# Diagonal masks on TensorE, the forget gate's place, and the order of emptying queries and keys in a two-branch attention layer

## The chip, the cores and the metric

The kernel runs on one core of a Trainium2 chip. The metric is the device time of one execution in microseconds (us), the median of several runs. A core has five engines with a queue of instructions each: TensorE (PE) for matmuls, VectorE (DVE), ScalarE (ACT), GpSimd (POOL), and SyncE (SP), which here only starts transfers. An engine runs its queue in order; engines wait for each other through semaphores. TensorE writes its results into eight PSUM banks of 128 x 512 floats, and ACT and DVE empty them.

## The reference

One decoder layer on 512 tokens of width 1024. Its mixing part has two causal attention branches of 8 heads with 64 channels each, forgetting attention (FoX) and stick-breaking attention (SB):

```
mod = c @ w_ada + b_ada                 # shift, scale and gate for both parts
u = x * (1.0 + sc1) + sh1
q_a, k_a, v_a, f_a, q_b, k_b, v_b, g_a, g_b = split(u @ w_in)
log_f = log_sigmoid(f_a + b_forget);  cum = cumsum(log_f)
y_fox = softmax(where(s <= t, q k^T / 8 + cum_t - cum_s, -inf)) @ v
z = q k^T / 8                                               # stick-breaking
log_one_minus = where(s < t, log_sigmoid(-z), 0)
rest = cumsum(log_one_minus, reversed over s) - log_one_minus
y_sb = where(s < t, exp(log_sigmoid(z) + rest), 0) @ v
merged = sigmoid(g_a) * (y_fox @ w_fox_proj) + sigmoid(g_b) * (y_sb @ w_sb_proj)
x = layer_norm(alpha * x + (1.0 + gt1) * (merged @ w_o))
...
```

After it comes a gated MLP with a causal depthwise convolution of width 3, and a second layer norm. Everything is in float32.

## The kernel before

Each float32 operand is split into a high part of reduced precision (`wh`, `uh`, `s`, `m`; ACT copies it, L75) and a low part, the rest (`wl`, `ul`; DVE subtracts, L78). A product is then three matmuls, high x high, low x high and high x low (L116 to L118).

The program has four stretches. Up to about 52 us the modulation is worked out and the first block of projections runs (L270). Up to about 300 us the attention runs. Then come the output projection and layer norm, the up projection (L116 to L118 on `u2h`), the down projection (L984 to L986) and the last norm.

The attention goes through 16 heads, the 8 SB heads first (pairs 0 to 3), then the 8 FoX heads (pairs 4 to 7). Each head has three stages. Stage a (L446) computes scores from `s` (queries) and `m` (keys) into three banks (L454 and L455). For an SB head ACT then takes two sigmoids, of -z into `om` and of z into `pt` (L487, L488); POOL sets the diagonal blocks of `pt` to zero above and on the diagonal (L490); DVE scans `om` from right to left for the running products (L493), and POOL multiplies (L494). For a FoX head four matmuls with `mska` (L460) add -1e30 above the diagonal, and a softmax follows. Stage b (L504) transposes the ten blocks of `pt` (L514) into three banks, which ACT empties into `ph`, `ptc` (high) and DVE into `pl`, `ptc` (low). Stage c (L527) multiplies by the values (L532); ACT and DVE add the two halves (`ytmp` L538, `yf` L539), and after a pair split the sum into `yh` and `yl`.

Between these stages `fill` pulls matmuls out of a `stream` of independent work: projections of queries and keys of later pairs, of the branch gates (`proj`), values (`vproj`, `vgroup`), the branches' output products (`bproj`), and two row sums of the modulation (`ada_sum`, L584 and L585, whose operands `ach` and `acl` are split by `ada_split`). `fill` takes a fixed number of triples (`FILL`), and the stream must have reached the next pair's keys before that pair's scores. Up to head 6's turn the stream stops ahead of `vgroup`, the values of the FoX heads, whose four banks are filled side by side with 96 matmuls (L428 to L430).

The stream's weights are items in one list. SP loads them in that order into four raw buffers, and DVE and ACT split them one or two items ahead of their use. Between them stand 24 modulation pieces (`add_ada`): the first 8 are added up on DVE in two `ac` sums (L561, L566), the others reduced against c (L170). `skip` counts how many places for a piece stay empty at first. The first two items (`EARLY`) are held back behind a given instruction. SP runs in the order of the code; the order on the four other engines is set by a scheduler from the dependencies, with `issue_after` as a hint, so a change in one place moves instructions in others.

`q_evac` and `k_evac` empty a pair's projection bank: rows 0 to 63 are the first head, rows 64 to 127 the second. ACT and DVE take turns on a bank. `forget` (the Abs, Exp and Ln of the forget gate on ACT, each with its table; its scan L328 and its split `chi` on DVE; rows sent into `s` and `m` of the FoX heads by POOL's transfers) is called ahead of head 4's turn.

Of the kernel before, what the change touches and what calls it, by code (L numbers as in the profile page):

```python
# [8 lines left out]
F32 = mybir.dt.float32  # L9
F32R = mybir.dt.float32r  # L10
BF16 = mybir.dt.bfloat16
AF = mybir.ActivationFunctionType
ALU = mybir.AluOpType
# [3 lines left out]
P = 128  # L17
# [9 lines left out]
NEG = -1.0e30  # L27
# [18 lines left out]
def layer_kernel(ctx: ExitStack, tc: tile.TileContext, out, xT, x, cT, crow, wa0, wa1, bcol, bgt, w1, wct, wv, bf,  # L46
# [3 lines left out]
    V, S, G, PE = nc.vector, nc.scalar, nc.gpsimd, nc.tensor  # L50
# [14 lines left out]
    def bank():  # L65
        return pp.tile([P, 512], F32, name=nm("ps"), tag="ps")

    def const(shape, dt, s):
        return cons.tile(shape, dt, name=s, tag=s)

    def fl(ap):
        return ap.bitcast(F32)
# [4 lines left out]
    def lo_of(o, i, hi):  # L77
        return V.tensor_tensor(o, i, fl(hi), ALU.subtract)  # L78
# [20 lines left out]
    identb = const([P, P], BF16, "identb")  # L99
    V.tensor_copy(identb, ident)  # L100
    zerob = const([P, P], BF16, "zerob")
    G.memset(zerob, 0.0)
    mska = const([P, P], BF16, "mska")
    G.affine_select(mska, zerob, pattern=[[-1, P]], compare_op=ALU.is_ge, fill=NEG, base=0, channel_multiplier=1)
    one = const([P, 512], F32, "one")
    G.memset(one, 0.0)
    G.affine_select(one[:, 384:512], one[:, 384:512], pattern=[[-1, P]], compare_op=ALU.is_gt, fill=1.0, base=0, channel_multiplier=1)
    bfs = const([NH, 1], F32, "bfs")
    modc = const([P, 4, KT], F32, "modc")
    modr = const([P, 4, KT, 2], F32, "modr")  # L110
# [11 lines left out]
    state = {"load": 0, "proc": 0}  # L122
# [17 lines left out]
    def process():  # L140
        it = items[state["proc"]]
        if state["proc"] < EARLY:
            with tc.issue_after(state["after"].ins):
                it[4] = it[1](it[3])
        else:
            it[4] = it[1](it[3])
        state["proc"] += 1
# [151 lines left out]

    OFS = ((0, 0), (2, 0), (0, 128), (1, 0))  # L300
    SEG = (((0, 128), (128, 512)), ((0, 512),), ((0, 256),))
    ptc = [[att.tile([P, 512], F32R, name=f"ptc{i}{e}", tag=f"ptc{i}{e}") for e in range(2)] for i in range(2)]
    for e in ptc:
        for t in e:
# [2 lines left out]
    m2t = [att.tile([68, 512], F32R, name=f"m2_{i}", tag=f"m2_{i}") for i in range(4)]  # L307
# [37 lines left out]
    hd = {}  # L345
# [3 lines left out]
    def slot_free(n):  # L349
        assert n < 4 or n - 4 in scored  # L350
        return n % 4

    def idx(br, h):
        return h if br == 1 else NH + h

    def q_evac(br, p, ps):
        for hh in range(2):
            h = 2 * p + hh
            r = slice(64 * hh, 64 * hh + 64)
            s1 = z(F32R, "s1")  # L360
            hi_of(s1[0:64, :], ps[r, :], 0.125)
            V.scalar_tensor_tensor(s1[64:128, :], ps[r, :], 0.125, fl(s1[0:64, :]), ALU.mult, ALU.subtract)
            d = hd.setdefault((br, h), {})
            d["s1"] = s1
            if br == 0:
                s2 = s2t[slot_free(idx(br, h))]
                hi_of(s2[0:64, :], ps[r, :], 0.125)
                d["s2"] = s2
            else:
                d["s2"] = s1  # L370

    def k_evac(br, p, ps):
        for hh in range(2):
            h = 2 * p + hh
            r = slice(64 * hh, 64 * hh + 64)
            m1 = z(F32R, "m1")
            hi_of(m1[0:64, :], ps[r, :])
            hi_of(m1[64:128, :], ps[r, :])
            m2 = m2t[slot_free(idx(br, h))]
            lo_of(m2[0:64, :], ps[r, :], m1[0:64, :])  # L380
            d = hd.setdefault((br, h), {})
            d["m1"], d["m2"] = m1, m2

    def v_evac(br, j, half, ps):
        vv = z(F32R, "vv")
# [59 lines left out]

    def stage_a(br, h):  # L446
        d = hd[(br, h)]
        bk = [bank(), bank(), bank()]

        def scores(i):  # L450
            b, o = OFS[i]
            w = max(256, (i + 1) * P)
            tb = slice(i * P, (i + 1) * P)
            PE.matmul(bk[b][:, o : o + w], d["s1"][:, tb], d["m1"][:, 0:w], start=True, stop=False)  # L454
            PE.matmul(bk[b][:, o : o + w], d["s2"][0:68, tb], d["m2"][0:68, 0:w], start=False, stop=br == 1)  # L455

        def mask(i):
            b, o = OFS[i]
            if br == 0:
                PE.matmul(bk[b][:, o + i * P : o + i * P + P], identb, mska, start=False, stop=True)  # L460

        scores(0)
        mask(0)
        scores(2)
        scores(1)
        scores(3)
        mask(2)
        mask(1)
        mask(3)
        pt = [z(F32, "pt"), z(F32, "pt"), z(F32, "pt")]  # L470
        if br == 0:
            sm = att.tile([P, 12], F32, name=nm("sm"), tag="sm", bufs=3)
            for i in (0, 2, 1, 3):
                b, o = OFS[i]
                c = slice(o, o + (i + 1) * P)
                V.tensor_reduce(sm[:, i : i + 1], bk[b][:, c], AX.X, ALU.max, negate=True)
                S.activation(pt[b][:, c], bk[b][:, c], AF.Exp, bias=sm[:, i : i + 1], accum_out=sm[:, 4 + i : 5 + i])
            V.reciprocal(sm[:, 8:12], sm[:, 4:8])
            for i in (0, 2, 1, 3):
                b, o = OFS[i]  # L480
                c = slice(o, o + (i + 1) * P)
                V.tensor_scalar_mul(pt[b][:, c], pt[b][:, c], sm[:, 8 + i : 9 + i])
        else:
            for b in (0, 2, 1):
                w = SEG[b][-1][1]
                om = z(F32, "om")
                S.activation(om[:, 0:w], bk[b][:, 0:w], AF.Sigmoid, scale=-1.0)  # L487
                d["last"] = S.activation(pt[b][:, 0:w], bk[b][:, 0:w], AF.Sigmoid)  # L488
                dg = pt[b].rearrange("p (a c) -> p a c", c=P)[:, (0, 3, 1)[b] : w // P : 3, :]
                G.affine_select(dg, dg, pattern=[[0, dg.shape[1]], [-1, P]], compare_op=ALU.is_gt, fill=0.0, base=0, channel_multiplier=1)  # L490
                for s, e in SEG[b]:
                    d0 = om[:, s + 1 : e][:, ::-1]
                    V.tensor_tensor_scan(d0, d0, one[:, 513 - (e - s) : 512][:, ::-1], 1.0, ALU.mult, ALU.max)  # L493
                    G.tensor_tensor(pt[b][:, s : e - 1], pt[b][:, s : e - 1], om[:, s + 1 : e], ALU.mult)  # L494
        d["pt"] = pt
        scored.add(idx(br, h))
        if br == 0 and h + 4 < NH:
            decay_rows(h + 4)
        if br == 1 and h >= 4 and gated:
            decay_rows(h - 4)  # L500
# [136 lines left out]
    stream, sums = [], []  # L637
    adas = [0]

    skip = [7]  # L640

    def add_ada(n=1):
        for _ in range(n):
            if skip[0]:
                skip[0] -= 1
            elif adas[0] < 24:
                add_item(wa1[adas[0]], ada_proc(adas[0]))
                adas[0] += 1
                if adas[0] in (4, 8):
                    stream.append((ada_split, (adas[0] // 4 - 1, len(items) - 1)))  # L650
                    sums.append([len(stream) + 1, adas[0] // 4 - 1])
# [34 lines left out]
    for p, ng in ((1, 0), (2, 0), (3, 2), (4, 1)):  # L686
        if p == 4:
            marks["v0"] = len(stream)
            for j in range(4):
                stream.append((vgroup, (j, add_item(wv[0, j], split_proc))))  # L690
                add_ada(2)
        add_pair(p)
        if p == 1:
            for j in range(4):
                wvi.append(add_item(wv[1, j], v_proc))
            for j in range(NB):
                stream.append((vproj, (1, j, wvi[-1])))
            marks["v1"] = len(stream)
        for _ in range(ng):
            add_gate(1, gb.pop(0))  # L700
# [80 lines left out]
    heads = [(br, 2 * p + e) for br, p in seq for e in range(2)]  # L781
    last = hd[heads[1]]['last']
    for n, (b, h) in enumerate(heads):
        if n == 4:
            forget(last)
        f1, f2, f3 = FILL[n // 8]
        if n + 2 < 16:
            if n == 6:
                lim[0] = marks["y1"]
            if n % 2 == 0:  # L790
                fill_to(marks[(n // 2 + 1, "k")])
            last = hd[heads[n + 1]].get("last")
            stage_a(*heads[n + 2])
        fill(f1)
        if n + 1 < 16:
            stage_b(*heads[n + 1])
        fill(f2)
        if n == 0:
            fill_to(marks["v1"])
        stage_c(b, h)  # L800
        if n == 7:
            lim[0] = marks["y0"]
        if n == 15:
            lim[0] = len(stream)
        fill(f3)
# [98 lines left out]
    hh, hl = [], []  # L904
# [34 lines left out]
    for n in range(2 * FT):  # L939
        if n < NSPLIT:  # L940
            h, l = items[wui[n]][4]
            ps = bks[n]
            up_mm(ps, h, l, slice(256, 512))
        else:
            ps = bank()
            h, l = weights(wui[n])
# [13 lines left out]
        if n % 2 == 1:  # L960
# [4 lines left out]
            a, b = z(F32R, "hh"), z(F32R, "hl")  # L965
# [23 lines left out]
    for j in range(FT - LATE):  # L989
        w = weights(wdi[j])  # L990
# [4 lines left out]
    for i in range(NB):  # L995
        tb = slice(i * P, (i + 1) * P)
        r = x1[i]
# [96 lines left out]
```

## Time and profile before

| what | value |
|---|---|
| median of three runs (770.62, 772.75, 772.47) | 772.47 us |
| the profiled execution | 773.12 us |
| its span, first to last instruction | 771.4 us |
| mean granted TensorE clock | 0.994 |
| TensorE busy | 752.7 us |
| DVE, ACT, POOL busy | 546.5, 350.9, 197.9 us |

The 1.7 us between the profiled execution and its span lie before the first and after the last instruction. A row of a timeline gives start, duration, engine, line, operation, output <- inputs and shapes; "x3" means that three equal rows in a row are taken together, and brackets give the time in which the engine stood idle just before, with what ended it. The program's names stand without their numbers.

### The profile page before, as it was taken

The numbers are of one execution on the slowest core, as the hardware profiler recorded it, in microseconds if no ns is written. First come the engines' busy times: TensorE is split into PE (matmuls) and PEld (weight loads), VectorE is DVE, ScalarE is ACT, GpSimd is POOL, SyncE is SP. The second block draws the span as 40 slices with busy tenths as digits, with TensorE's granted clock in tenths as the row PEclk, the third lists the DMA queues.
The fourth block names the chain that finished last, engine by engine and source line by source line (L and its number), as shares of the span: only waits on it lengthen the run. The fifth ranks groups of instructions, "written<-read, shape, count | busy, mean of one in ns | idle before, by whom it ended". The sixth has DMA issues, their size and how long they took to land.

```text
span 771.4 us, 9543 instructions
## 1 busy us (share of the span) xinstructions
PE 752.7 (98%) x3538; PEld 622.3 (81%) x3538; DVE 546.5 (71%) x816; ACT 350.9 (45%) x587; POOL 197.9 (26%) x162
## 2 busy tenths in 40 slices
PE   8999999898999999999999999999999999999995
PEld 4877888786888888888889888888888888888885
DVE  6868668988789885776676787677656665534666
ACT  3568468725867555433145434444444433222300
POOL 1037236920100011363000780000000043945500
PEclk9999999999999999999999999999999999999999
DMA  8952310378332323455302524344332214322302
GB/s 330 405 181 82 110 56 28 111 243 274 112 113 92 121 86 123 155 166 163 137 1 71 204 76 146 119 178 137 112 106 93 100 54 165 122 96 88 105 27 83
DMA packets 31106, 99.68 MB, mean 129 GB/s; under 512 B 4274, under 2 KB 4786, under 8 KB 31059
## 3 DMA queue, kind: packets, MB, share of 16 engines
q1 hardware_dynamic: 30258, 98.72, 37.3%
q8 instruction: 28, 0.46, 0.3%
q10 hardware_dynamic: 288, 0.28, 0.1%
q0 software_dynamic: 512, 0.07, 0.1%
q14 instruction: 20, 0.16, 0.1%
HBM read 96.88 MB, written 2.10 MB: 128 GB/s over the span
## 4 chain that ended last, share of the span: by engine, by line
PE 83%; DVE 7%; ACT 5%; DMA 3%; issue 2%; DVEq 0%; ACTq 0%
PE ps L116 16%; PE ps L117 16%; PE ps L118 16%; PE ps L985 5%; PE ps L986 5%; PE ps L984 5%; PE ps L270 4%; PE ps L532 2%; PE ps L864 2%; PE ps L863 2%; PE ps L865 2%; PE ps L514 2%; DVE wl L78 1%; PE ps L454 1%; DVE om L493 1%
## 5 line engine op out<-in xcount | busy, mean ns | idle before, releaser
L78 DVE TENSOR_TENSOR wl<-raw,wh 128x1024 fp32r<-128x1024 f32 (+2 forms) x106 | 147.1, 1389 | 92.4 <-ACT wh L75 91.9
L75 ACT ACTIVATE wh<-raw 128x1024 fp32r<-128x1024 f32 (+2 forms) x106 | 110.3, 1042 | 98.7 <-PE ps L986 38.3
L116 PE MATMUL ps<-u2h,wh 128*128 128x512 f32 (+1 forms) x376 | 141.4, 376 | 0.0
L117 PE MATMUL ps<-u2l,wh 128*128 128x512 f32 (+1 forms) x376 | 141.3, 376 | 0.0
L118 PE MATMUL ps<-u2h,wl 128*128 128x512 f32 (+1 forms) x376 | 141.3, 376 | 0.0
L624 POOL TENSOR_TENSOR raw<-raw,gt 128x1024 f32<-128x1024 f32 x22 | 59.7, 2727 | 190.8 <-DVE gt L587 157.7
L117 PEld LDWEIGHTS ps<-u2l,wh 128*128 128x128 f32 x376 | 70.8, 188 | 12.9
L116 PEld LDWEIGHTS ps<-u2h,wh 128*128 128x128 f32 x376 | 70.8, 188 | 12.8
L118 PEld LDWEIGHTS ps<-u2h,wl 128*128 128x128 f32 x376 | 70.8, 188 | 12.6
L116 PE MATMUL ps<-uh,wh 128*128 128x512 f32 x200 | 79.7, 399 | 0.0
L117 PE MATMUL ps<-ul,wh 128*128 128x512 f32 x200 | 78.5, 392 | 0.0
L118 PE MATMUL ps<-uh,wl 128*128 128x512 f32 x200 | 78.4, 392 | 0.0
L985 PE MATMUL ps<-wl,hh 128*128 128x512 f32 x128 | 49.9, 390 | 0.0
L986 PE MATMUL ps<-wh,hl 128*128 128x512 f32 x128 | 49.8, 389 | 0.0
L984 PE MATMUL ps<-wh,hh 128*128 128x512 f32 x128 | 49.8, 389 | 0.0
L118 PEld LDWEIGHTS ps<-uh,wl 128*128 128x128 f32 x200 | 37.7, 189 | 8.1
L116 PEld LDWEIGHTS ps<-uh,wh 128*128 128x128 f32 x200 | 37.8, 189 | 7.1
L117 PEld LDWEIGHTS ps<-ul,wh 128*128 128x128 f32 x200 | 37.9, 189 | 6.9
L75 ACT ACTIVATE hh<-cv 128x512 fp32r<-128x512 f32 x22 | 13.9, 632 | 59.8 <-DVE cv L964 59.8
L612 POOL TENSOR_TENSOR raw<-raw,gt 128x1024 f32<-128x1024 f32 x8 | 19.9, 2498 | 78.2 <-DMA raw<-in_wo 47.2
L963 ACT ACTIVATE cv<-cv 128x512 f32<-128x512 f32 x22 | 13.9, 632 | 54.6 <-DVE cv L958 54.6
L494 POOL TENSOR_TENSOR pt<-pt,om 128x127 f32<-128x127 f32 (+3 forms) x32 | 34.5, 1088 | 1.8
(192 smaller groups left out, 1532.3 us busy)
## 6 DMA issues: line engine op xcount, KB each, us to landing
raw<-in_wup SPq DMA_DIRECT2D x44, 512.0 KB, 3.3
raw<-in_wa SPq DMA_DIRECT2D x32, 512.0 KB, 3.4
raw<-in_wct SPq DMA_DIRECT2D x25, 512.0 KB, 4.0
raw<-in_wdn SPq DMA_DIRECT2D x22, 512.0 KB, 3.3
wa<-in_wa SPq DMA_DIRECT2D x14, 512.0 KB, 7.9
raw<-in_wv SPq DMA_DIRECT2D x8, 512.0 KB, 3.9
raw<-in_wp SPq DMA_DIRECT2D x8, 512.0 KB, 3.4
raw<-in_wo SPq DMA_DIRECT2D x8, 512.0 KB, 3.2
```

The source lines that it names most:

```text
L75: S.activation(o, i, AF.Copy, scale=scale)
L78: return V.tensor_tensor(o, i, fl(hi), ALU.subtract)
L116: PE.matmul(ps, wh, ah, start=first, stop=False)
L117: PE.matmul(ps, wh, al, start=False, stop=False)
L118: PE.matmul(ps, wl, ah, start=False, stop=last)
L270: PE.matmul(grp[g], w, u, start=j == 0 and n == 0, stop=j == KT - 1 and n == (1 if g == 7 else 2))
L494: G.tensor_tensor(pt[b][:, s : e - 1], pt[b][:, s : e - 1], om[:, s + 1 : e], ALU.mult)
L612: G.tensor_tensor(r, r, gt[0], ALU.mult)
L624: G.tensor_tensor(r, r, gt[1], ALU.mult)
L984: PE.matmul(ps, hh[j][:, tb], w[0], start=first, stop=False)
L985: PE.matmul(ps, hh[j][:, tb], w[1], start=False, stop=False)
L986: PE.matmul(ps, hl[j][:, tb], w[0], start=False, stop=last)
```

## The change

The diff, cut to its core:

```diff
-    one = const([P, 512], F32, "one")
-    G.memset(one, 0.0)
-    G.affine_select(one[:, 384:512], one[:, 384:512], pattern=[[-1, P]], compare_op=ALU.is_gt, fill=1.0, base=0, channel_multiplier=1)
+    mskb = const([P, P], BF16, "mskb")
+    G.affine_select(mskb, zerob, pattern=[[-1, P]], compare_op=ALU.is_gt, fill=NEG, base=0, channel_multiplier=1)
...
         if state["proc"] < EARLY:
-            with tc.issue_after(state["after"].ins):
+            with tc.issue_after(state["k" if state["proc"] else "after"].ins):
...
     def q_evac(br, p, ps):
         for hh in range(2):
...
             hi_of(s1[0:64, :], ps[r, :], 0.125)
-            V.scalar_tensor_tensor(s1[64:128, :], ps[r, :], 0.125, fl(s1[0:64, :]), ALU.mult, ALU.subtract)
...
+        for hh in range(2):
+            r = slice(64 * hh, 64 * hh + 64)
+            s1 = hd[(br, 2 * p + hh)]["s1"]
+            V.scalar_tensor_tensor(s1[64:128, :], ps[r, :], 0.125, fl(s1[0:64, :]), ALU.mult, ALU.subtract)

     def k_evac(br, p, ps):
         for hh in range(2):
...
             hi_of(m1[0:64, :], ps[r, :])
             hi_of(m1[64:128, :], ps[r, :])
-            m2 = m2t[slot_free(idx(br, h))]
-            lo_of(m2[0:64, :], ps[r, :], m1[0:64, :])
             d = hd.setdefault((br, h), {})
-            d["m1"], d["m2"] = m1, m2
+            d["m1"], d["m2"] = m1, m2t[slot_free(idx(br, h))]
+        for hh in range(2):
+            r = slice(64 * hh, 64 * hh + 64)
+            d = hd[(br, 2 * p + hh)]
+            state["k"] = lo_of(d["m2"][0:64, :], ps[r, :], d["m1"][0:64, :])
...
     def stage_a(br, h):
+        msk = mska if br == 0 else mskb
...
-            PE.matmul(bk[b][:, o : o + w], d["s2"][0:68, tb], d["m2"][0:68, 0:w], start=False, stop=br == 1)
+            PE.matmul(bk[b][:, o : o + w], d["s2"][0:68, tb], d["m2"][0:68, 0:w], start=False, stop=False)
         def mask(i):
             b, o = OFS[i]
-            if br == 0:
-                PE.matmul(bk[b][:, o + i * P : o + i * P + P], identb, mska, start=False, stop=True)
+            PE.matmul(bk[b][:, o + i * P : o + i * P + P], identb, msk, start=False, stop=True)
...
-                dg = pt[b].rearrange("p (a c) -> p a c", c=P)[:, (0, 3, 1)[b] : w // P : 3, :]
-                G.affine_select(dg, dg, pattern=[[0, dg.shape[1]], [-1, P]], compare_op=ALU.is_gt, fill=0.0, base=0, channel_multiplier=1)
                 for s, e in SEG[b]:
                     d0 = om[:, s + 1 : e][:, ::-1]
-                    V.tensor_tensor_scan(d0, d0, one[:, 513 - (e - s) : 512][:, ::-1], 1.0, ALU.mult, ALU.max)
+                    V.tensor_tensor_scan(d0, d0, zer.broadcast_to([P, e - s - 1]), 1.0, ALU.mult, ALU.add)
...
-    skip = [7]
+    skip = [2]
...
                 stream.append((vgroup, (j, add_item(wv[0, j], split_proc))))
-                add_ada(2)
+                add_ada()
...
-        if n == 4:
+        if n == 6:
             forget(last)
```

The SB heads now get their diagonal from four matmuls each with `mskb`, -1e30 on and above the diagonal, so that both sigmoids come out as 0 and 1 there; 24 selects on POOL go, and the scan adds a zero where it took a maximum before. Six modulation pieces (one before) stand ahead of `vgroup` and four (eight before) in it. A projection's high parts are emptied for both heads before the low parts. The second early item's split is held back behind the first pair's last low key part.

On DVE the instructions between head 6's scans and the low parts of its transposed weights stand, before, in this order. `om` are the scans, the last `pl` is head 6's:

```order
L493 SCALAR_TENSOR_TENSOR om_1508<-om_1508,one 128x127
L493 SCALAR_TENSOR_TENSOR om_1508<-om_1508,one 128x383
L566 SCALAR_TENSOR_TENSOR ac_264_1360<-raw_1588,cTs,ac_264_1360 128x512
L493 SCALAR_TENSOR_TENSOR om_1516<-om_1516,one 128x255
L493 SCALAR_TENSOR_TENSOR om_1522<-om_1522,one 128x511
L566 SCALAR_TENSOR_TENSOR ac_264_1360<-raw_1588,cTs,ac_264_1360 128x512
L78 TENSOR_TENSOR pl_1546<-ps_1540,ph_1545 128x512
```

These are head 7's scans; ahead of them stand head 5's low parts, one ac, a wl and a yf. In the change the same stretch, from head 5's last low part to head 6's pl (pl_1564), is this (modr and modc: a modulation row, L169):

```order
L78 TENSOR_TENSOR pl_1458<-ps_1453,ph_1457 128x384
L570 SCALAR_TENSOR_TENSOR ac_269_1384<-raw_1382,cTs,ac_269_1384 128x512 x2
L570 SCALAR_TENSOR_TENSOR ac_269_1384<-raw_1497,cTs,ac_269_1384 128x512 x2
L570 SCALAR_TENSOR_TENSOR ac_269_1384<-raw_1630,cTs,ac_269_1384 128x512
L543 TENSOR_TENSOR yf_1490<-ps_1481,ytmp_1491 64x512
L570 SCALAR_TENSOR_TENSOR ac_269_1384<-raw_1630,cTs,ac_269_1384 128x512
L328 SCALAR_TENSOR_TENSOR fq_548<-fq_548,fq_547 8x512
L329 SCALAR_TENSOR_TENSOR fq_547<-ones,fq_548 8x512
L169 SCALAR_TENSOR_TENSOR raw_1664,modr<-raw_1664,cbc 128x1024
L497 SCALAR_TENSOR_TENSOR om_1532<-om_1532,zer 128x127
L497 SCALAR_TENSOR_TENSOR om_1532<-om_1532,zer 128x383
```

After these two rows come the other two scans of head 7 and pl_1564. Six ac rows stand ahead of it where there were three; the forget gate's two and a modulation row have come, and the wl has gone.

On ACT, ahead of pair 3's keys (m_260 and m_261, of which pair 3's first scores need the first two), this stood before:

```order
L75 ACTIVATE ph_1314<-ps_1310 128x384
L75 ACTIVATE chi<-fq_546 8x512
L75 ACTIVATE wh_1465<-raw_1358 128x1024
L538 ACTIVATE ytmp_1342<-ps_1333 64x512
L75 ACTIVATE yh_1345<-yf_1232 128x512
L75 ACTIVATE m_260_1349<-ps_1245 64x512 x2
L75 ACTIVATE m_261_1353<-ps_1245 64x512 x2
```

And this in the change:

```order
L75 ACTIVATE ph_1332<-ps_1328 128x384
L75 ACTIVATE ptc_518<-ps_1336 128x384
L75 ACTIVATE wh_1501<-raw_1495 128x1024
L542 ACTIVATE ytmp_1360<-ps_1351 64x512
L75 ACTIVATE yh_1363<-yf_1245 128x512
L75 ACTIVATE m_262_1367<-ps_1258 64x512 x2
L75 ACTIVATE m_263_1370<-ps_1258 64x512 x2
L75 ACTIVATE ach_1377<-ac_140_772 128x512
```

`chi` has left this place, and `ach`, the high part of the first row sum, has come behind the keys; the order of the rest is the same.

More of the change, by code (lines that the diff above doesn't have):

```diff
@@ L301, in layer_kernel @@
     SEG = (((0, 128), (128, 512)), ((0, 512),), ((0, 256),))
+    zer = const([P, 1], F32, "zer")
+    G.memset(zer, 0.0)
     ptc = [[att.tile([P, 512], F32R, name=f"ptc{i}{e}", tag=f"ptc{i}{e}") for e in range(2)] for i in range(2)]
```

## The prediction

> **What bounds the kernel now.** First the page: busy shares, then the chain of work that ended last.
>
> ```profile
> PE 752.7 (98%) x3538; PEld 622.3 (81%) x3538; DVE 546.5 (71%) x816; ACT 350.9 (45%) x587; POOL 197.9 (26%) x162
> PE 83%; DVE 7%; ACT 5%; DMA 3%; issue 2%; DVEq 0%; ACTq 0%
> ```
>
> TensorE is busy for 752.7 of 771.4 us and carries 83% of the chain. So an edit counts only by the instructions that it gives TensorE, and by the moments in which TensorE stands or runs slow. POOL, at 26%, costs nothing by being busy. Next, the table of 20 us windows (PE, PEld, DVE, ACT, POOL busy, then granted clock) shows where TensorE is not full:
>
> ```profile
> 120.00:140.00 20.00, 17.90 (x88) 15.06 (x88) 16.10 (x23) 16.38 (x28) 12.74 (x18) 0.93 0.19 59
> 140.00:160.00 20.00, 19.05 (x97) 16.01 (x96) 19.90 (x26) 12.50 (x25) 17.50 (x18) 0.98 0.38 128
> 180.00:200.00 20.00, 16.97 (x77) 13.21 (x76) 17.72 (x35) 10.96 (x23) 1.07 (x2) 0.91 0.72 231
> ```
>
> TensorE's waits from 40 us on name what was late (us in total, times, longest):
>
> ```profile
> PE ps L454 <- ACT m L75: 4.1, 2, 2.1
> PE ps L585 <- DVE acl L78: 1.1, 1, 1.1
> PE ps L412 <- DVE wvl L78: 1.0, 1, 1.0
> PE ps L428 <- DVE pl L78: 1.0, 1, 1.0
> PE ps L411 <- ACT wvh L75: 0.5, 2, 0.3
> ```
>
> I call them A (the two on wvl and wvh, near 68 us), B and E (the two on m: first scores of pairs 3 and 5), C (the value weights of the filling stretch, held by pl) and D (acl). The timeline of TensorE shows B, E and what follows E:
>
> ```profile
> 136.77 0.82 PE L454 MATMUL ps<-m,s 128*128 128x256 f32 x3 [2.10 <-ACT m L75]
> 191.93 1.22 PE L454 MATMUL ps<-m,s 128*128 128x256 f32 x3 [1.98 <-ACT m L75]
> 192.95 0.63 PE L116 MATMUL ps<-uh,wh 128*128 128x512 f32 x1
> 193.38 0.63 PE L117 MATMUL ps<-ul,wh 128*128 128x512 f32 x1
> ```
>
> After E the 512-wide matmuls start 0.43 us apart, elsewhere 0.23 (231.48 to 231.71 below). The windows agree: a clock of 0.91 over 20 us loses 1.8 us, 0.93 loses 1.4. So idle times of 2.10 and 1.98 us brought some 1.6 us each of half clock behind them, and the waits of 1.0 and 1.1 brought none. B and E cost 2.1+1.6 and 2.0+1.6, A 1.5, C 1.0, D 1.1: 10.9 us in all is what the change could win.
>
> **Masks on TensorE: +2.9.** Scores of a stick-breaking head (no masks), then of a forgetting head (four masks), each up to the next projection; and the price of a mask alone on both engines:
>
> ```profile
> 121.19 0.28 PE L454 MATMUL ps<-m,s 128*128 128x256 f32 x1
> 122.49 0.40 PE L116 MATMUL ps<-uh,wh 128*128 128x512 f32 x1
> 229.58 0.28 PE L454 MATMUL ps<-m,s 128*128 128x256 f32 x1
> 231.17 0.47 PE L116 MATMUL ps<-uh,wh 128*128 128x512 f32 x1
> 231.48 0.39 PE L117 MATMUL ps<-ul,wh 128*128 128x512 f32 x1
> 231.71 0.40 PE L118 MATMUL ps<-uh,wl 128*128 128x512 f32 x1
> L460 PE MATMUL ps<-mska,identb 128*128 128x128 bf16 x32 | 4.6, 226 | 0.0
> L490 POOL TENSOR_SCALAR_AFFINE_SELECT pt<-pt 128x256 f32<-128x256 f32 x8 | 10.2, 1272 | 28.9 <-ACT pt L488 28.8
> ```
>
> 1.59 us (229.58 to 231.17) less 1.30 is 0.29 for four masks, and the next matmul is 0.31 to its successor instead of 0.23: 0.37 a head, 2.9 for eight. Bounds: 2.3 without the tail, 4.6 if the busy time of L460 counts whole. The selects taken from POOL give nothing by themselves, since no wait of TensorE names POOL; at most they stop slowing DVE (below).
>
> **B: -3.1.** What made m late:
>
> ```profile
> 123.08 1.28 ACT L326 ACT_TABLE_LOAD   x1
> 126.48 1.21 DVE L328 TENSOR_TENSOR_SCAN fq<-ones,fq 8x512 f32<-8x512 f32 x1
> 132.20 0.59 ACT L538 ACTIVATE ytmp<-ps 64x512 f32<-64x512 f32 x1
> 133.05 1.20 DVE L78 TENSOR_TENSOR wl<-raw,wh 128x1024 fp32r<-128x1024 f32 x1
> 134.28 0.69 DVE L539 TENSOR_TENSOR yf<-ps,ytmp 64x512 f32<-64x512 f32 x1
> 135.01 0.63 ACT L75 ACTIVATE yh<-yf 128x512 fp32r<-128x512 f32 x1 [2.23 <-DVE yf L539]
> 135.55 1.17 ACT L75 ACTIVATE m<-ps 64x512 fp32r<-64x512 f32 x2
> ```
>
> ACT's queue holds yh ahead of m; yh waits for yf, and yf stands on DVE behind the forget scan, chi and wl. The change takes the forget gate away from here: two table loads of 1.28 ahead of head 5's sigmoids on ACT, a scan, fq and chi of some 2.6 us on DVE, so DVE reaches wl and yf some 3 to 4 us earlier. But only 15 projection matmuls, 3.4 us, are now left between the last values product and these scores, where 24 were before. In that time must pass a ytmp 0.59, yf 0.69, yh 0.63 and the two high halves 1.17: 3.1 and handovers. Just in time; I leave 0.6 of 3.7. Bounds: 0 left, or all of it. That the scores start on one head's high part and the low parts come after all four high ones (about 1.2 later) costs pairs 2 and 5 some 0.4 each, **+0.8**: the row of 191.93 shows three matmuls on high parts first, and with the projections and transposes put between they cover about 1.6 of the 2.0 us from a first high pair to the first low part (1.2 more of high parts, 0.1, 0.69).
>
> **E: -2.9, D: -1.1, A: -0.9.** For E:
>
> ```profile
> 188.05 1.20 ACT L75 ACTIVATE s<-ps 64x512 fp32r<-64x512 f32 x2 [2.06 <-DVE s L362]
> 190.69 1.19 ACT L75 ACTIVATE m<-ps 64x512 fp32r<-64x512 f32 x2
> ```
>
> ACT waited 2.06 us for the low part of the other head in the same bank, and m came out 2.06 too late; with all high parts first this wait is gone, and 0.8 of rest is left for the low parts. The second early weight's low part, now behind the first k's low parts, I cost at nothing: the first weight's 24 matmuls, 5.5 us at 0.23, cover its 1.2; without them it is 1.2. D goes because acl is computed a stage earlier, A shrinks since DVE reaches wvl earlier; of these I have the order of the instructions alone, and bound each by zero gain and the whole wait.
>
> **C: +4.1.** The gate's work and five of the modulation steps now stand on DVE between head 6's low transposes and the work before them. The fourth bank of the value weights waits, as before, for head 6's pl to leave its bank. DVE, from head 6's first scan:
>
> ```profile
> 127.62 3.26 DVE L493 TENSOR_TENSOR_SCAN om<-om,one 128x127 f32<-128x127 f32 x4
> 143.61 0.69 DVE L78 TENSOR_TENSOR pl<-ps,ph 128x512 fp32r<-128x512 f32 x1
> 145.14 0.85 DVE L566 SCALAR_TENSOR_TENSOR ac<-raw,cTs,ac 128x512 f32<-128x512 f32 x1
> 145.92 2.11 DVE L78 TENSOR_TENSOR wl<-raw,wh 128x1024 fp32r<-128x1024 f32 x1
> 188.05 1.23 DVE L170 SCALAR_TENSOR_TENSOR raw<-raw,cbc 128x1024 f32<-128x1024 f32 x1
> ```
>
> Four scans 3.26, gt 0.69, pl-ptc-pl 1.53 (143.61 to 145.14), six ac 5.1, yf 0.69, fq 0.69 and its scan 1.21, a modulation row 1.23, head 7's scans 3.26, pl 0.69: 18.4, starting 0.7 after head 6's scores. TensorE, from these scores to the fourth bank:
>
> ```profile
> 124.59 1.25 PE L514 MATMUL ps<-ident,pt 128*128 128x128 f32 x10
> 125.60 0.48 PE L116 MATMUL ps<-uh,wh 128*128 128x512 f32 x1
> 127.75 0.56 PE L532 MATMUL ps<-ph,vv 128*128 128x512 f32 x2
> 129.04 0.40 PE L116 MATMUL ps<-uh,wh 128*128 128x512 f32 x1
> ```
>
> Ten transposes 1.01, values 1.29. So: six transposes 0.6, 6 projections 1.4, two 512-wide 0.5, values 1.3, 9 projections 2.05, head 7's scores 1.67, 9 projections 2.05, transposes 1.0, 6 projections 1.4, values 1.3, eleven of the value matmuls 2.5: 15.7. TensorE comes 3.4 too early. As after B and E I add 1.6 of half clock and 0.1: 5.1, against 1.0 before. Bounds: DVE's queue 1 us shorter (six ac at the 0.69 of other 512-wide rows) and TensorE held 1 us elsewhere leave 1.4, no half clock; slowed as wl was by POOL's work (2.11 at 145.92, 1.20 at 133.05) on a few rows, or with the late load of the modulation row, 6 and 1.6. ACT's extra table load of 1.28 hides there: head 7's sigmoids still come before DVE gets to their scans.
>
> [...]
>
> **Sum.** +2.9 -3.1 +0.8 -2.9 -1.1 -0.9 +4.1 = -0.2 on the profiled execution's 773.12: 772.9 us. That execution lies 0.65 above the median of the runs shown, 772.47; a median of the changed kernel may lie as much lower, which the range takes in.
>
> **Rivals.** About 0.3% (2.3 us) is what a measurement tells from no change.
> 1. No change, 772.9 (own range 770.3 to 774.8): 0.42. For it: gains and costs rest on the same kind of rows.
> 2. Slower: the high parts still come late at B and E, because ACT's in-order queue has yh (B) or a weight's high part (E) ahead of them. It decides once DVE's yf is over 0.5 us later than the 3.4 us of cover allow. One such wait of 2 us brings back its half clock: 772.9+3.1 = 776.0, both 778.9. For it: 15 projections instead of 24. Against it: the forget work is gone from there. 0.2.
> 3. Slower: DVE is slowed in C as at 145.92; a 6 us stop gives 772.9+2.6 = 775.5, and with the mask at 4.6 us 777.2. 0.14.
> 4. Faster: C's stop stays under about 1.5 us, with no half clock: 772.9-3.6 = 769.3; with D, A and E gone whole 768. For it: 1.0 there before, and DVE may run its rows without POOL beside it. Against it: the count above. 0.24.
>
> Faster 0.24, same 0.42, slower 0.34. The range, 768.6 to 777.6, leaves out the ends of 2 and 4.
>
> **What would show it.** The row of four masks between scores and projection at 0.3 us, POOL's 20 us of selects gone. Waits of TensorE on m under 1 us with no half clock near 135 and 190 us; one long wait on pl near 150 us with a clock under 1 behind it, and pl behind head 7's scans on DVE. I am wrong if that wait is short, if the waits on m are still there, or if a new wait of over 1 us, on a low part or a load, stands elsewhere.

## The result and the profile after

The changed kernel takes 775.39 us (median of 20 runs, 773.44 to 777.4) against 772.71 us of the kernel before (20 runs beside them). The ratio is 1.0029, with a 95% interval of 1.0018 to 1.0040: 0.3% slower, and clear of zero. The forecast was 772.9, and it had let "no change" end at 774.8.

The page of the changed kernel, busy shares by engine:

```profile
PE 755.8 (98%) x3570; PEld 622.2 (80%) x3570; DVE 546.7 (71%) x816; ACT 352.4 (46%) x588; POOL 180.8 (23%) x138
```

TensorE has 32 more matmuls and is busy 3.1 us longer; POOL has lost the 24 selects. The span is 773.7 us where it was 771.4. The windows of the changed kernel (columns as before):

```profile
120.00:140.00 20.00, 19.41 (x109) 16.01 (x108) 17.45 (x24) 14.21 (x27) 9.47 (x9) 1.00 0.16 53
140.00:160.00 20.00, 16.17 (x85) 13.19 (x84) 19.79 (x29) 18.40 (x31) 9.81 (x9) 1.00 0.42 132
160.00:180.00 20.00, 20.00 (x83) 16.33 (x82) 14.23 (x23) 5.20 (x8) 4.34 (x8) 0.91 0.65 202
180.00:200.00 20.00, 19.41 (x95) 15.57 (x94) 16.26 (x31) 10.63 (x19) 1.03 (x2) 1.00 0.65 221
```

The two stretches that were thin before (17.90 at 120, 16.97 at 180) are nearly full now. The one at 140 has fallen from 19.05 to 16.17, and the clock is low in the window behind it. TensorE's waits from 40 us on, whole, say why:

```profile
PE ps L434 <- DVE pl L78: 3.8, 1, 3.8
PE ps L461 <- ACT m L75: 1.3, 3, 0.6
PE ps L418 <- DVE wvl L78: 1.0, 2, 0.7
PE ps L461 <- DVE m L78: 0.6, 1, 0.6
PE ps L462 <- DVE m L78: 0.4, 1, 0.4
PE ps L868 <- DVE wol L78: 0.2, 1, 0.2
```

And its timeline places them:

```profile
56.04 0.35 PE L461 MATMUL ps<-m,s 128*128 128x256 f32 x1 [0.57 <-DVE m L78]
135.92 0.74 PE L461 MATMUL ps<-m,s 128*128 128x256 f32 x3 [0.52 <-ACT m L75]
159.11 0.50 PE L434 MATMUL ps<-wh,uh 128*128 128x512 f32 x1 [3.83 <-DVE pl L78]
160.50 0.63 PE L435 MATMUL ps<-wl,uh 128*128 128x512 f32 x1
160.93 0.63 PE L436 MATMUL ps<-wh,ul 128*128 128x512 f32 x1
193.88 0.74 PE L461 MATMUL ps<-m,s 128*128 128x256 f32 x3 [0.15 <-ACT m L75]
197.30 0.38 PE L462 MATMUL ps<-m,s 68*128 68x256 f32 x1 [0.43 <-DVE m L78]
270.32 0.73 PE L461 MATMUL ps<-m,s 128*128 128x256 f32 x3 [0.61 <-ACT m L75]
```

B fell from 2.10 to 0.52 and E from 1.98 to 0.15, both without half clock; D is gone. C went from 0.95 to 3.83, with the 0.43 us spacing of half clock behind it. Four short waits are new: 0.57 at the first scores, 0.43 on a low part behind E, 0.61 at pair 7's scores, and 0.2 on a weight of the output projection.

Corrections of names: E is at the first scores of the FoX heads, which is pair 4 by the count used for the kernel; the prediction and the expectations say "pair 5" for it throughout. And the scans at 127.62, which the prediction gives as head 6's, run ahead of head 6's scores (136.77) and are head 5's; it took only their length from them.

### The profile page after: what moved, and what is told of

It reads as the page before. It is cut to its first block, busy times and chain, and to the rows that moved or that the text cites. A ratio compares the mean times of both kernels' runs of the same rounds, so it can differ in the third digit from the quotient of the medians.

```text
span 773.7 us, 9591 instructions
## 1 busy us (share of the span) xinstructions
PE 755.8 (98%) x3570; PEld 622.2 (80%) x3570; DVE 546.7 (71%) x816; ACT 352.4 (46%) x588; POOL 180.8 (23%) x138
## 4 chain that ended last, share of the span: by engine, by line
PE 79%; DVE 10%; DMA 4%; ACT 3%; issue 2%; POOL 0%; SPq 0%; DVEq 0%; ACTq 0%; POOLq 0%
PE ps L115 15%; PE ps L116 15%; PE ps L117 15%; PE ps L989 5%; PE ps L990 5%; PE ps L988 5%; PE ps L269 4%; DMA raw<-in_wa 2%; PE ps L536 2%; ACT m L75 1%; PE ps L868 1%; PE ps L869 1%; PE ps L867 1%; PE ps L518 1%; DVE wl L78 1%
## 5 line engine op out<-in xcount | busy, mean ns | idle before, releaser
L498 POOL TENSOR_TENSOR pt<-pt,om 128x127 f32<-128x127 f32 (+3 forms) x32 | 38.3, 1226 | 41.0 <-ACT pt L494 29.7
```

## The experiments

Each kernel ran beside the kernel before, on the same chip; the ratios are to that. The changed kernel's is 1.0029. e1 to e4, e5 to e8 and e9 to e12 ran on one chip each, so times of different groups are compared by these ratios.

### Which part of the change costs what

The first four take one part out of the changed kernel.

```diff
# e1: stage_a, the scan and the constant of the kernel before, so
+                G.affine_select(dg, dg, pattern=[[0, dg.shape[1]], [-1, P]], compare_op=ALU.is_gt, fill=0.0, base=0, channel_multiplier=1)
# e2
-        if n == 6:
+        if n == 4:
             forget(last)
# e3
-    skip = [2]
+    skip = [7]
-                add_ada()
+                add_ada(2)
# e4: q_evac and k_evac of the kernel before
```

> The changed kernel with the stick-breaking diagonal back on POOL (selects, scan with a maximum); all else as changed. Theory (each term is worth what it takes from TensorE's time): 32 masks are 8 x 0.37 = 2.9 us, so about 772.5 us, 0.3% under the changed kernel, and the stop on pl in the filling stretch stays at 3.8 us or a little less. Rival (the selects kept DVE's scans free of POOL's multiplies or slowed them): then the stop on pl itself changes by over 0.7 us, with the scans of heads 6 and 7 3.26 instead of 3.75 us each, and the gain is more than 3.5 or less than 2.

Measured: 772.24 us, ratio 0.9993 (0.9973 to 1.0014). Against 1.0029 that is 0.36%, 2.8 us, beside the 2.9 of the theory (the two intervals leave some 1.8 us either way); the stop on pl is 3.70. The rival falls: the scans do get shorter, 3.17 instead of 3.75 us for four, but the stop hardly moves, since TensorE also comes earlier without the masks.

> The changed kernel with the forget gate back at head 4's turn. Theory (the stop of 3.8 us on pl and 1.8 us of half clock come from DVE's queue of gate, modulation sums and head 7's scans): the queue ahead of pl is shorter by six rows, the stop falls under 1 us without half clock, -4.6; the scores of pair 3 get some wait on m back, +1 to +3.7: 771.5 to 774.5 in all. Rival (the filling stretch has slack later, so a stop taken away there comes back at pair 4's scores): 775, with a new wait on m or a low part behind the filling stretch.

Measured: 776.44 us, ratio 1.0037 (1.0021 to 1.0053). The rival holds. The stop on pl is down to 1.57, without half clock, and a new one stands at the first FoX scores. DVE's timeline, and TensorE's row behind it:

```profile
194.41 1.23 DVE L169 SCALAR_TENSOR_TENSOR raw<-raw,cbc 128x1024 f32<-128x1024 f32 x1 [3.19 <-DMA raw<-in_wa]
195.67 1.41 DVE L78 TENSOR_TENSOR m<-ps,m 64x512 fp32r<-64x512 f32 x2
196.41 0.58 PE L462 MATMUL ps<-m,s 68*128 68x256 f32 x1 [2.85 <-DVE m L78]
```

DVE stood 3.19 us for a modulation row's load, with the low parts of the keys queued behind it. The clock lost another 3.4 us there (0.89 and 0.94 in two windows). In the changed kernel the same row, at 195.29, waited 1.42 for its load and TensorE 0.43: the long stop upstream had given the load time.

> The changed kernel with the modulation pieces where they were (one ahead of the value weights, eight among them). Theory: DVE's queue ahead of pl is about 14 us against TensorE's 15, so the stop falls under 1 us, without half clock, -4.6; the waits on the second row sum's low part (1.1) and on m of pair 5 stay or come back, +1 to +3: 771 to 773.5. Rival (the gate alone makes the queue too long, by ACT's four table loads ahead of head 7's sigmoids): the stop stays over 2 us, 774 to 775.5.

Measured: 767.85 us, ratio 0.9928 (0.9907 to 0.9950), better than either theory said, and faster than both kernels. The waits and the two windows that had been low:

```profile
PE ps L418 <- DVE wvl L78: 1.1, 2, 0.7
PE ps L462 <- DVE m L78: 0.7, 1, 0.7
PE ps L461 <- DVE m L78: 0.6, 1, 0.6
PE ps L461 <- ACT m L75: 0.5, 1, 0.5
PE ps L434 <- DVE pl L78: 0.4, 1, 0.4
140.00:160.00 20.00, 19.64 (x101) 16.23 (x100) 19.62 (x26) 18.66 (x30) 10.91 (x13) 1.00 0.33 106
180.00:200.00 20.00, 19.14 (x100) 15.47 (x99) 19.43 (x42) 15.46 (x28) 1.57 (x4) 1.00 0.69 217
```

3.3 us of waits where the changed kernel has 7.3, and no half clock, 1.8 there: 5.8 of some 7.8 us (1.01%). The expected return of 1 to 3 us at the second row sum and at the keys did not come: that sum's wait is absent, and 0.7 is all that is left at the keys.

> The changed kernel with queries and keys emptied head by head as before. Theory (the high parts of both heads first is what ended pair 5's wait of 2.0, while the gate's move ended pair 3's): pair 5's wait comes back with its half clock, +3.6, less the waits of 0.4 to 0.6 on low parts, -1: 778. Rival (both waits went by the gate's move and the pieces' move): no wait of over 1 us on m, about 774.5.

Measured: 774.46 us, ratio 1.0014 (0.9999 to 1.0030). The rival is near. The stop on pl got longer, and E came back only in part:

```profile
159.08 0.74 PE L429 MATMUL ps<-wh,uh 128*128 128x512 f32 x1 [4.68 <-DVE pl L78]
193.81 0.74 PE L456 MATMUL ps<-m,s 128*128 128x256 f32 x3 [1.04 <-ACT m L75]
```

So in the changed kernel the emptying order gains nothing. With the old order m still comes late at E, at 192.57 us where it was 190.69 before; but TensorE, behind the masks and the stop of 4.68, comes there at 192.77 instead of 189.95, and so waits little.

### Each part alone, put into the kernel before

The next run leaves out both losing parts; the three behind it put one part alone into the kernel before.

```diff
# e5: e1 and e3 together
# e6, the kernel before with: q_evac and k_evac of the change
# e7, the kernel before with
-        if n == 4:
+        if n == 6:
             forget(last)
# e8, the kernel before with
-    skip = [7]
+    skip = [2]
-                add_ada(2)
+                add_ada(1)
```

> The changed kernel with both the pieces back where they were and the diagonal back on POOL: of the change there stay the gate at head 6's turn and the emptying order. Theory (masks and pieces are separate losses): the 767.85 us of the run with the pieces back, less 2.9 for the masks: 765.0. Rival (with the selects on POOL and no masks, TensorE reaches the fourth bank of the value weights earlier and stops there): a stop of 1.5 to 2.5 us on pl, up to 1.6 of half clock, 766.5 to 768.5.

Measured: 766.91 us, ratio 0.9915 (0.9893 to 0.9937). This lies in the rival's range, 0.13% under e3 and not the 0.36% that the masks cost in e1, though the intervals overlap. But no stop on pl took the rest, as the rival has it: the wait at that matmul is 0.41, and the profile puts it down to ACT's pt. The scores of pair 4 took it:

```profile
187.38 0.71 PE L459 MATMUL ps<-m,s 128*128 128x256 f32 x3 [0.84 <-DVE s L373]
190.53 0.38 PE L460 MATMUL ps<-m,s 68*128 68x256 f32 x1 [1.31 <-DVE m L78]
186.55 1.41 DVE L373 SCALAR_TENSOR_TENSOR s<-ps,s 64x512 fp32r<-64x512 f32 x2
189.80 1.40 DVE L78 TENSOR_TENSOR m<-ps,m 64x512 fp32r<-64x512 f32 x2
```

DVE is busy 19.20 of 20 us in that window, and reaches the low parts when it can. TensorE, earlier by the masks, waits 2.15 there against 0.74 in e3. (The profiled execution is the slowest of e5's six, 768.81 us, by what lies ahead of these rows: its first scores start at 57.02, in e3 at 55.45.)

> The kernel before with the new emptying order alone. Theory (this order ends pair 5's wait, the gate's move ends pair 3's): pair 5's 2.0 with its half clock goes, -3.6, pair 3's stays, some 1.0 to 1.5 of short waits on low parts come: 770 to 770.5. Rival (with the gate in place the order ends neither, as it was worth nothing in the changed kernel, 774.46 against 775.39): 772 to 773.

Measured: 771.65 us, ratio 0.9970 (0.9955 to 0.9985): a gain of 0.30%, 2.3 us, near the theory's 2.2 to 2.7 rather than the rival's nothing. E is down to 0.78, on a low part. The two longest waits left, and the windows that hold them:

```profile
71.51 0.51 PE L417 MATMUL ps<-wvl,uh 128*128 128x512 f32 x1 [1.76 <-DVE wvl L78]
157.58 0.50 PE L433 MATMUL ps<-wh,uh 128*128 128x512 f32 x1 [2.01 <-DVE pl L78]
60.00:80.00 20.00, 18.05 (x78) 14.60 (x78) 16.89 (x19) 14.56 (x27) 10.49 (x12) 0.91 0.29 90
140.00:160.00 20.00, 16.53 (x83) 13.53 (x84) 19.91 (x26) 13.38 (x25) 18.33 (x22) 1.00 0.38 133
```

The wait of 1.76 was followed by half clock, the one of 2.01 was not (1.00 in its window and in the next). The hold on the second early item's split, which the change has and this kernel has not, was not tried alone; the longest wait on wvl is 1.1 us in the kernels with it.

B fell to 0.95 here with the gate still in its old place, which the theory had not said. It did not fall because m came sooner. On ACT, m stands behind chi, which waits for the gate's scan:

```profile
136.14 0.63 ACT L75 ACTIVATE chi<-fq 8x512 fp32r<-8x512 f32 x1 [0.56 <-DVE fq L328]
136.68 2.39 ACT L75 ACTIVATE m<-ps 64x512 fp32r<-64x512 f32 x4
```

That is 1.1 us later than in the kernel before (135.55). But TensorE, behind the 1.76 and its half clock, comes 2.3 us later, at 136.95 instead of 134.67.

> The kernel before with the forget gate's move alone. Theory (the gate's work delays DVE and with it pair 3's keys): pair 3's wait falls from 2.1 to under 0.6 and its half clock goes, -3.2; the stop on pl grows from 1.0 to 1 to 1.7 (DVE's queue 16 us against TensorE's 15), no half clock: 769 to 770. Rival (the move alone makes the long stop on pl): a stop over 2 us with half clock, 773 to 775.

Measured: 770.45 us, ratio 0.9963 (0.9946 to 0.9979). B is 0.79 and C 1.51, both without half clock, as the theory has them; but E grew:

```profile
152.64 0.51 PE L428 MATMUL ps<-wh,uh 128*128 128x512 f32 x1 [1.51 <-DVE pl L78]
190.54 0.80 PE L454 MATMUL ps<-m,s 128*128 128x256 f32 x2 [3.33 <-ACT m L75]
```

What TensorE won at B it waits for again, in part, at E, where the old emptying order still stands.

> The kernel before with the pieces' move alone. Theory (the move makes the stop on pl only together with the gate's move, but by itself puts a modulation row whose load comes late ahead of pair 5's low key part): pl's stop under 1 us, the wait on the second row sum's low part (1.1) gone, a wait on a low key part of pair 5 of 1.5 to 3 us in place of 2.0 on m: 771.5 to 775. Rival (the pieces are what cost 7.5 us in any company): 779 to 780.

Measured: 778.03 us, ratio 1.0054 (1.0033 to 1.0076), nearer the rival. C is gone (not among the waits), and yet its ratio is the highest of all:

```profile
137.01 0.74 PE L454 MATMUL ps<-m,s 128*128 128x256 f32 x3 [2.11 <-ACT m L75]
192.56 0.80 PE L454 MATMUL ps<-m,s 128*128 128x256 f32 x2 [4.59 <-ACT m L75]
273.94 0.39 PE L455 MATMUL ps<-m,s 68*128 68x256 f32 x1 [1.74 <-DVE m L78]
180.00:200.00 20.00, 15.41 (x67) 12.39 (x66) 15.07 (x29) 11.24 (x23) 1.07 (x2) 0.83 0.52 172
```

E is 4.59 and its half clock 3.4 us, so the pieces' move is a loss by itself, without the gate and without the long stop on pl. What the move won at C and D, 2.0 us, TensorE waits for again at E: it comes there at 187.97 instead of 189.95, and m comes 0.6 later than before (191.31 against 190.69).

### What makes the stop on pl, and the pieces' places

```diff
# e9, the changed kernel with
-                if k > 0:
+                if k == 1:
...
# e10, the changed kernel with
-    skip = [2]
+    skip = [7]
# e11, e3 with the first pair emptied by the kernel before's q_evac and k_evac, kept as
-    q_evac(1, 0, grp[0])
-    k_evac(1, 0, grp[1])
+    q_evac0(1, 0, grp[0])
+    k_evac0(1, 0, grp[1])
# e12, e5 with the first pair as in e11, and
-    skip = [7]
+    skip = [6]
```

> The changed kernel with the ac sums cut to their first step (12 of the 14 multiply-adds of the two gate rows are left out, so the gates' values are not the reference's); gate, masks and emptying order as changed, the pieces' loads in their new places. Theory (the stop on pl is as long as DVE's queue ahead of it exceeds TensorE's work): without six ac of 0.76 the queue is about 15.4 us with its start against TensorE's 15.6, so the stop of 3.83 falls under 0.8 and the half clock of 1.8 us goes; of the 7.5 us that putting the pieces back gave, 5 to 5.5 come here: 770 to 770.5. Rival (it is the loads and rows brought forward, not the sums): the stop stays over 2 us, 774 to 775.

Measured: 770.95 us, ratio 0.9967 (0.9950 to 0.9983), and the stop:

```profile
155.85 0.50 PE L434 MATMUL ps<-wh,uh 128*128 128x512 f32 x1 [0.94 <-DVE pl L78]
```

0.94, without half clock. The loads stood where the change puts them and the gate stood where it does; the sums on DVE alone made the difference: 0.62%, 4.8 us. (The run leaves out nearly all steps of both sums, not only the six ahead of pl.)

> The changed kernel with the five pieces ahead of the value weights taken back there, and one piece instead of two kept beside each value weight. Theory (the stop comes from the sums ahead of the value weights): DVE's queue is as with all pieces back, the stop under 1 us: 768 to 769.5, a little more where the rows left over stand before a low key part. Rival (fewer pieces beside the value weights are what costs): 773 or more, with the wait of over 1.5 us on m or a low part of pair 5, 6 or 7.

Measured: 770.80 us, ratio 0.9962 (0.9945 to 0.9979). The stop on pl is 0.34, so it is the pieces ahead of the value weights that make it. The rest, 0.34% or 2.6 us over e3, is neither theory's. It is lost in the output projection, whose weights come behind the pieces in the list; from its first matmul to the up projection's first it takes 48.9 us, 46.1 in e3:

```profile
364.60 0.51 PE L867 MATMUL ps<-woh,mh 128*128 128x512 f32 x1 [0.90 <-ACT woh L75]
```

> The run with the pieces back, with the first pair alone emptied head by head as before. Theory (the wait of 0.56 us at the first scores is the price of putting the low parts last where TensorE has nothing else to do): that wait goes, -0.5: 767.3, no other place changes. Rival (the old order brings back a wait on m there or delays wvl): 767.8 to 769.

Measured: 767.90 us, ratio 0.9924 (0.9899 to 0.9948), the same as e3. The 0.56 at the first scores became 0.33, on a memset of POOL, and pair 4's keys waited 0.38 and 0.97. The wait was there, but TensorE only carried it to the next place.

> Gate at head 6's turn, new emptying order but for the first pair, diagonal on POOL, two pieces ahead of the value weights and eight among them. Theory (DVE's queue ahead of pl holds no sum here and is about 12 us; TensorE saves the masks' 2.9): no stop on pl, and pair 5's low key part is the one wait of over 1 us left: 764.5 to 766. Rival (as with masks off and pieces back, what the masks free is given back at the next low part): 766.5 to 767.5.

Measured: 768.75 us, ratio 0.9946 (0.9925 to 0.9967). No stop on pl, as expected, but B was back:

```profile
135.19 0.79 PE L487 MATMUL ps<-m,s 128*128 128x256 f32 x2 [3.30 <-ACT m L75]
133.42 0.63 ACT L75 ACTIVATE yh<-yf 128x512 fp32r<-128x512 f32 x1 [4.56 <-DVE yf L572]
120.00:140.00 20.00, 16.70 (x79) 14.14 (x78) 18.01 (x24) 10.11 (x19) 7.53 (x9) 0.85 0.43 137
```

One more piece, begun earlier, has put two ac steps ahead of yf on DVE, and yh holds ACT's queue ahead of m, the chain of the prediction's B with another cause in front. The lowest ratio of all is e5's, 0.85% under the kernel before; the intervals of e3 and e11 overlap with it.

## Why the prediction was right, and where it was not

**The masks**, +2.9: measured 2.8 (e1 against the change), with about as long a stop on pl (3.70 us in e1, 3.83 in the change) and about the same mean clock over their executions (0.995 and 0.994). With the pieces back their price is not seen whole: e5 is only 0.13%, 1.0 us, under e3, since most of the rest is waited for at pair 4.

**B**, -3.1 with 0.6 left: 0.52 left, no half clock. In the change, yf stands 2.9 us behind the start of the last values product ahead of these scores, where it stood 6.5 behind it before (127.75 to 134.28): 3.6 earlier, and the text had 3 to 4.

```profile
130.52 0.56 PE L536 MATMUL ps<-ph,vv 128*128 128x512 f32 x2
133.42 0.69 DVE L543 TENSOR_TENSOR yf<-ps,ytmp 64x512 f32<-64x512 f32 x1
```

So the mechanism is as predicted, and e7, with the gate moved alone, has 0.79. But the gate is not the only way to a long or a short wait here. Other work ahead of yf made it 3.30 in e12. With the gate at its old place it was 0.95 in e6 and 0.93 in e2, where not yf but chi held m, and TensorE came some 2 us later than in the kernel before.

**C**, +4.1: this term decided, and it came out as counted, step by step. DVE in the changed kernel:

```profile
140.23 3.75 DVE L497 TENSOR_TENSOR_SCAN om<-om,zer 128x127 f32<-128x127 f32 x4
146.15 3.89 DVE L570 SCALAR_TENSOR_TENSOR ac<-raw,cTs,ac 128x512 f32<-128x512 f32 x5
154.26 3.75 DVE L497 TENSOR_TENSOR_SCAN om<-om,zer 128x127 f32<-128x127 f32 x4
158.38 0.68 DVE L78 TENSOR_TENSOR pl<-ps,ph 128x512 fp32r<-128x512 f32 x1
```

From 140.23 to 159.06 it is 18.8 us against 18.4 reckoned: the scans took 0.5 more each time than the 3.26 used, the ac 0.75 rather than 0.85. The stop was 3.83 against 3.4, the half clock 1.8 against 1.6. On TensorE it is 16.0 us from the end of head 6's scores (139.26) to the stop (155.28), against 15.7 reckoned. That it comes from the sums is shown by e9 and e10. They are one half of it: with the sums in place and the gate back at its old place (e2) the stop is 1.57, without half clock.

**E**, -2.9, and **D**, -1.1: E fell by more, to 0.15 and 0.43 for its low part, and D went. The step that named the cause was incomplete, though. High parts first is worth 2.3 us in the kernel before (e6), where E fell to 0.78; in the changed kernel E would have been only 1.04 without it (e4), because C's stop and the masks bring TensorE there 2.8 us later. E and C are not independent terms: in e7, with B's time won and C at 1.51, E is 3.33. D is in no run but the kernel before, also where the pieces stay at their old places (e6, e7), so their move is not what it takes to end it.

**A**, -0.9: from 1.5 to 1.0, half of that. **Low parts**, +0.8 at pairs 2 and 4: 0.43 at pair 4, none at pair 2, but 0.57 at the very first scores, where the text had no term, and 0.61 for the high part at pair 7.

**The sum.** Waits and half clock were 7.7 and 3.6 us before (the windows' 0.93, 0.98 and 0.91), and are 7.3 and 1.8 after: 2.2 us won, where the terms had 3.1 (-0.2 without the masks). With the masks' 2.8 that makes +0.6. The span grew by 2.3. Of the 1.7 left, 0.5 is there ahead of the attention: the last matmul of the first block starts at 50.31 in the kernel before and at 50.83 in the change; in the other kernels it lies between 50.26 and 51.82, so one profile tells nothing of it. Another 0.5 lies between the first matmul of the output projection and the first of the up projection, 46.1 us before and 46.6 after, and the other kernels but e10 have 46.1 to 46.7 there. The remaining 0.7 was not settled.

The half clock of a profile is that of one execution, too. The profiled execution of the change has a granted clock of 0.996, as high as any of its 20, which lie between 0.992 and 0.996; their mean is 0.994. In 79 executions of the kernel before it lies between 0.989 and 0.998, and the mean is 0.994 as well. So over all executions the change wins no clock on average, where the profiles show 1.8 us and the terms have 1.6. The waits' 0.4 less and the masks' 2.8 then make +2.4, near the measured 2.2 (by the ratio) to 2.7 (by the medians). This is an estimate: it takes the waits of one profile for those of all.

So the mechanism was right, several waits traded for one longer one, and the middle of the forecast was 2.5 us low. The waits came out 0.9 worse than the terms: C by 0.6, A by 0.4, the short waits by 0.4, with B and E some 0.6 better; the other 1.7 had no term. The measured time is above the 774.8 that the forecast gave to no change, and inside its whole range only by the room left for the slower rivals, neither of which happened as described: in this the forecast was lucky. Rival 3 named 775.5, near the measured time, but by a stop of 6 us that did not occur. Rival 4, a stop on pl under 1.5 us, is what e9, e10 and e3 have, and they are 0.6 to 1.0% faster than the change.

The pieces' move, which the prediction treated as a part of C alone, is the losing part: 1.0% in the changed kernel (e3), 0.54% in the kernel before (e8). It costs twice over, as sums ahead of pl, and as rows whose loads come late in front of the first FoX keys (e2, 3.19 us).

## What to carry to other kernels

An edit that shortens a wait on one engine's queue moves the consumer forward, and the next producer with little slack becomes the wait (E, 1.98 us before, was 3.33 in e7 and 4.59 in e8): terms at different places do not add, so the best version has to be found by taking parts out again, and here that was worth 1.1%. When filler work is moved to an earlier place, count it on the in-order queue that also frees the buffers of the critical engine; DVE, busy for 19.9 of 20 us in that window before, had no room for three more sums, the gate's rows and a modulation row. Ask which waits a stop upstream is hiding before it is removed.

## What the runs showed of the hardware

Half clock (512-wide matmuls 0.43 us apart, elsewhere 0.23) follows some short idle times of TensorE and not others. In the profiled executions, idle times of 1.76 (e6), 1.98 and 2.10 us (before) had it behind them; 2.01 (e6) and 2.11 (e8) had none, nor had 1.51 (e7) and 1.57 (e2). Those of 2.85 (e2), 3.30 (e12), 3.33 (e7), 3.83 (the change), 4.59 (e8) and 4.68 us (e4) all had it. The price, worked out as the 20 us of a window times what its granted clock lacks of 1, came in two sizes: 1.6 to 1.8 us (before, the change, e4, e6, e7), and 3.4 us (e2, e8, e12), whatever the idle time: 4.68 us cost 1.6 in e4 (windows of 0.98 and 0.94), and 2.85 cost 3.4 in e2 (0.89 and 0.94). What decides whether it comes, and in which size, no run shows. The clock also differs between executions of one kernel: e6's twelve have 0.994 to 0.998, and the profiled one, with half clock behind its 1.76, is the lowest.

The four scans of a head took different times from head to head, and the operation does not decide which. Head 7's took 3.75 in the change and 3.17 in e1, with a maximum instead of the added zero; but with a maximum they took 3.75 in e7, with an added zero head 6's took 3.12 in e9, and the first head's took 2.94 in both kernels:

```profile
58.93 2.94 DVE L497 TENSOR_TENSOR_SCAN om<-om,zer 128x127 f32<-128x127 f32 x4
```

What slows some of them was not tried.
